# A decoder layer on one Trainium2 core: its opening stage in a new order, with part of the w_mod sums on TensorE

## The chip, the core and the metric

One core of one Trainium2 chip runs the whole program. The metric is the device time of one execution in microseconds; a kernel's time is the median of several runs. Traces come from one profiled execution each, whose own time is given beside the runs'.

## The reference

One decoder layer for 256 tokens of width 2048, all in float32:

```python
c_act = silu(c)
mod = c_act @ w_mod + b_mod                      # (2048) @ (2048, 6*2048)
shift1, scale1, gate1, shift2, scale2, gate2 = split(mod, 6)
u = rms(x, norm1_w) * (1 + scale1) + shift1
proj = u @ w_in                                  # 18464 columns
# stick-breaking attention and gated DeltaNet from proj, merged by gates, w_out, then
u = rms(h, norm2_w) * (1 + scale2) + shift2
h = h + gate2 * ((silu(u @ w_gate) * (u @ w_up)) @ w_down)
```

What matters here is the start: no column of `proj` can be computed before a part of u is known, and a part of u needs x, its row norm, and the columns of shift1 and scale1 that belong to it, each a sum over all 2048 rows of w_mod.

## The kernel before

All large products are made on TensorE from a high and a low part: an operand is split into a float32r value (hi) and the rest (lo), and a product is hi·hi + lo·hi + hi·lo, three matmuls. The weights are read in loads `raw` of 512 KB (two K tiles of 128 rows by 512 columns) on SP's queue, the first two on SP and the next two on POOL (L297 to L312). ScalarE makes `wh` from a load (`split_hi`, L302), VectorE `wl` (`split_lo`, L307). Four buffers of each stand ready; the load for step n+4 is issued behind wl of step n. A step is one such load: two K tiles of one job, 24 matmuls. A job is 512 columns of one weight over all its K tiles.

The first jobs need u by K tiles, and u comes in four pieces of four K tiles (`PIECES`). So they run K outermost (`outer`, L985 and around): first three jobs over K tiles 0 to 7, whose sums are then parked in SBUF (`park`, L955; 12 steps), then three other jobs over all 16 K tiles (24 steps). A hook of the first job of each group calls `u_piece(pi)` (L492): pieces 0 and 1 at K tiles 0 and 4 of the first group, 2 and 3 at K tiles 8 and 10 of the second (`HK` is by how many tiles a hook comes early).

For one piece, `u_sums` (L413) goes through 16 blocks of w_mod: 128 rows by 512 columns of shift and 512 of scale, 512 KB each, loaded on POOL's queue into nine buffers `smod` (`load_smod`, L397, L407), up to eight ahead. VectorE adds each block, times its 128 values of c, to one of two accumulators in turn, acc01 and accb (the first two blocks by a plain multiply, L425, the others by L427 with the helper of L124). Then TensorE sums over the partitions: a matmul of each 128 accumulator columns with 64 columns of ones (`pb_mod`, L429 to L436), two of a piece's four column groups at a time, and three small VectorE steps make `mcols`, the scale and shift columns. `u_piece` applies them on ScalarE to xT (x normed and transposed), casts to uh on ScalarE, takes ul on VectorE (L498 to L504), and at once makes the piece's share of b and a (`pb_ba`).

In program order the opening is: constants and the small rows (L134 to L154), silu(c), the sums of blocks 0 to 3 (`NS0`), then the loads of x (`xs`, L447), `wba` (L449, 2048 rows of 128 bytes), `crow` (L451), `adt` (L453), the transposes of crow and their copy `cw` (L457 to L461), the squares of x, the root `rstd1` on POOL (L173), the scaling of x on VectorE (L471), the sums of blocks 4 to 7 (`NS1`), the transposes of x and their copies (L479, L480), the split of wba.

The order on each engine isn't the program's: the framework's scheduler lists the instructions per engine by its own picture of when they become ready, and goes by program order among those that are ready. `tc.keep_in_program_order(ins)` pins an instruction behind the one that was written before it on the same engine. Each engine takes its list in order. `tps`, `wp`, `big` and `ps` are pools of buffers; `bank` gives one of four PSUM banks of tag ms.

The 16 blocks' sums of the next piece are spread over the steps (in `run_jobs`):

```python
if n < n_outer and sums:
    next(sums[0], None)
    if tick % 3 == 0:
        next(sums[0], None)
```

Of the kernel before, what the change touches and what calls it, by code (L numbers as in the profile page):

```python
# [16 lines left out]
P = 128  # L17
# [21 lines left out]
H2 = 5  # L39
RG = 2  # L40
SMA = 8
NS0 = 4
NS1 = 4
PIECES = ((0, 4), (4, 4), (8, 4), (12, 4))
HK = (0, 0, 0, 2)
HOP = 3
LAG = 6
SBR = 16
# [49 lines left out]
def body(tc, cst, x, c, w_mod, b_mod, norm1_w, w_in, q_norm_w, k_norm_w, conv_w, a_log, dt_bias,  # L98
# [19 lines left out]
        nc.tensor.matmul(o, lhsT=lhsT, rhs=rhs, start=start, stop=stop, skip_group_check=True)  # L118

    def tt(o, a, b, op):  # L120
        nc.vector.tensor_tensor(out=o, in0=a, in1=b, op=op)  # L121

    def stt(o, a, s, b, op0, op1, **kw):
        nc.vector.scalar_tensor_tensor(out=o, in0=a, scalar=s, in1=b, op0=op0, op1=op1, **kw)  # L124

    def act(o, i, f, **kw):
        nc.scalar.activation(out=o, in_=i, func=f, **kw)

    def f32(t):
        return t.bitcast(F32)  # L130
# [158 lines left out]
    def run_jobs(jobs, bg_every=0, outer=(), bg_from=0):  # L289
# [11 lines left out]

        def split_hi(n):  # L302
            wh = wp.tile([P, 2, 512], F32R, tag="wh", name="wh", bufs=WB)
            nc.scalar.copy(out=wh, in_=raws[n])  # L304
            splits[n] = (wh,)

        def split_lo(n):  # L307
            wl = wp.tile([P, 2, 512], F32R, tag="wl", name="wl", bufs=WB)
            wh = splits[n][0]
            tt(wl, raws.pop(n), f32(wh), ALU.subtract)  # L310
            if n + RAWS < ns:
                load(n + RAWS)  # L312
            splits[n] = (wh, wl)
# [79 lines left out]

    loads = [(pi, g) for pi, (k0, kn) in enumerate(pieces) for g in range(KT * kn // 4)]
    smod = {}

    def load_smod(n):  # L397

        for i in [i for i in loads if i not in smod][:max(0, n - len([i for i in smod if smod[i] is not None]))]:
# [10 lines left out]
                    nc.gpsimd.dma_start(out=t[:, v], in_=src[:, v, :, c0:c0 + cn])  # L410
            smod[i] = t

    def u_sums(pi):  # L413
        k0, kn = pieces[pi]
        c0, cn = k0 * P, kn * P
        kg = 4 // kn
        for g in range(KT // kg):
            load_smod(SMA)
            t = smod[pi, g]
            smod[pi, g] = None  # L420
            for kk in range(kg):
                k = kg * g + kk
                a = (acc01, accb)[k % 2][:, :, c0:c0 + cn]
                if k < 2:
                    nc.vector.tensor_scalar(out=a, in0=t[:, :, kk], scalar1=cc[:, k:k + 1], scalar2=None, op0=ALU.mult)  # L425
                else:
                    stt(a, t[:, :, kk], cc[:, k:k + 1], a, ALU.mult, ALU.add)  # L427
            yield
        for i0 in range(0, kn, 2):  # L429
            pm = bank("pb_mod")  # L430
            for n in range(2):
                for i in range(2):
                    o = pm[:, 64 * (4 * n + i):64 * (4 * n + i + 1)]
                    sl = slice(c0 + (i0 + i) * P, c0 + (i0 + i + 1) * P)
                    mm(o, acc01[:, n, sl], ones[:, 0:64], True, False)
                    mm(o, accb[:, n, sl], ones[:, 0:64], False, True)  # L436
            kr = slice(k0 + i0, k0 + i0 + 2)
            tt(mcols[:, 0, kr], pm[:, 256:384:64], bsc1[:, kr], ALU.add)
            stt(mcols[:, 0, kr], mcols[:, 0, kr], 1.0, n1c[:, kr], ALU.add, ALU.mult)
            tt(mcols[:, 1, kr], pm[:, 0:128:64], bsh1[:, kr], ALU.add)  # L440
        yield

    sums = [u_sums(0)]
    for _ in range(NS0):
        next(sums[0])
    xs = big.tile([P, NB, D], F32, tag="s16", name="xs")
    nc.sync.dma_start(out=xs, in_=xv)  # L447
    wba = tps.tile([P, KT, 32], F32, name="wba")
    nc.sync.dma_start(out=wba, in_=w_in[:, OFF_BA:OFF_BA + 32].rearrange("(k p) n -> p k n", p=P))  # L449
    for i in range(2):  # L450
        nc.sync.dma_start(out=crow[:, i], in_=conv_w.rearrange("a (k p) -> (a k) p", p=P)[i * 96:(i + 1) * 96])  # L451
    adt = cp.tile([P, 2, H], F32, name="adt")
    nc.sync.dma_start(out=adt[:, 0], in_=a_log.partition_broadcast(P))  # L453
    nc.sync.dma_start(out=adt[:, 1], in_=dt_bias.partition_broadcast(P))

    cw = cp.tile([P, 2, 96], F32, name="cw")
    pc = bank("pb_cw")  # L457
    for i in range(2):
        nc.tensor.transpose(pc[:, i * 96:(i + 1) * 96], crow[:, i], ident[:96, :96])
    nc.vector.tensor_copy(out=cw, in_=pc[:, 0:192])  # L460
    cwv = cw.rearrange("p a b -> p (a b)")  # L461

    ss = cp.tile([P, 4, 8], F32, name="ss")
    xT = s16("xT")
    rstd1 = cp.tile([P, 2], F32, name="rstd1")
    for b in range(NB):
        act(xT[:, b * 8:(b + 1) * 8].rearrange("p k t -> p (k t)"), xs[:, b], AF.Square, accum_out=ss[:, 0, b:b + 1])
    nc.vector.tensor_scalar(out=ss[:, 1, 0:2], in0=ss[:, 0, 0:2], scalar1=1.0 / D, scalar2=EPS, op0=ALU.mult, op1=ALU.add)
# [22 lines left out]

    def u_piece(pi):  # L492
        k0, kn = pieces[pi]
        for _ in sums.pop():
            pass
        if pi + 1 < len(pieces):
            sums.append(u_sums(pi + 1))
        for k in range(k0, k0 + kn, 2):  # L498
            for i in range(2):
# [5 lines left out]
        if not pba:  # L505
# [904 lines left out]
```

## Time and profile before

| | |
|---|---|
| time, median of 3 runs | 2054.28 us (2053.36 to 2054.73) |
| the profiled execution: time | 2056.12 us |
| its span | 2054.1 us |
| TensorE busy (matmul) | 1983.1 us, 97% |
| VectorE busy | 1386.4 us, 67% |
| ScalarE busy | 1064.9 us, 52% |
| GpSimd busy | 108.9 us, 5% |
| mean granted TensorE clock | 0.99 |
| DMA | 449.72 MB, mean 219 GB/s |

How to read it: the rows further down come from one profiled execution. PE is TensorE's matmuls, PEld its weight loads, DVE VectorE, ACT ScalarE, POOL GpSimd, SP SyncE; a name with q behind it is that engine's instruction queue, where DMAs are issued. Starts and windows are microseconds from the span's start. L118 and the like are lines of the kernel; L118, L121, L124 and L127 are the helpers for matmul, tensor-tensor, scalar-tensor-tensor and activation, so a group is told apart by its operands. In square brackets stands how long the engine had been idle and what ended that. One fp32 matmul with ones appears as two records.

### The profile page before, as it was taken

The page shows a single profiled execution, that of the slowest core. Times are in us where ns is not written, and L with a number is a line of the kernel's source. Part 1 is how long each engine was busy: PE and PEld are TensorE (multiplying, and loading weights), DVE is VectorE, ACT ScalarE, POOL GpSimd, SP SyncE. Part 2 cuts the span into 40 slices and gives each one's busy share as a digit, 9 for nine tenths or more (in the row PEclk, how much of TensorE's full clock was granted, in tenths as well). Part 3 has the DMA queues.
Part 4 walks back from the last instruction along what each step waited for, and adds up shares of the span by engine and source line. Part 5 has one row for each costly group of instructions (what it writes and reads, how often), then busy time and mean ns, then how long its engine had stood idle before and what let it go on. Part 6 is the DMA issues. An engine that isn't in the chain of part 4 may idle for free.

```text
span 2054.1 us, 29271 instructions
## 1 busy us (share of the span) xinstructions
PE 1983.1 (97%) x11097; PEld 1720.7 (84%) x11097; DVE 1386.4 (67%) x1846; ACT 1064.9 (52%) x1766; POOL 108.9 (5%) x141
## 2 busy tenths in 40 slices
PE   1999999999999999999999999999999999999998
PEld 1899999897888888888888888788888888888887
DVE  4986979877676667447776877676775555556554
ACT  3346676776666667443454445554455334445432
POOL 4311011010000000000000000000000000000000
PEclk9899999999999999999999999999999999999999
DMA  8995533444776675768797888587875566665564
GB/s 302 386 336 184 160 126 116 125 122 142 240 229 197 223 232 165 222 193 284 253 309 257 301 320 277 178 269 239 268 244 185 195 193 188 188 189 186 186 214 134
DMA packets 208555, 449.72 MB, mean 219 GB/s; under 512 B 16103, under 2 KB 16538, under 8 KB 207902
## 3 DMA queue, kind: packets, MB, share of 16 engines
q1 hardware_dynamic: 198910, 413.25, 62.6%
q0 software_dynamic: 9504, 34.61, 4.5%
q8 instruction: 87, 1.43, 0.3%
q14 instruction: 54, 0.44, 0.1%
HBM read 445.70 MB, written 2.10 MB: 218 GB/s over the span
## 4 chain that ended last, share of the span: by engine, by line
PE 93%; DMA 3%; DVE 2%; issue 1%; ACT 1%; POOL 0%; SPq 0%; DVEq 0%; ACTq 0%; POOLq 0%
PE acc L118 85%; DMA smod<-in_w_mod 1%; DMA crow<-in_conv_w 1%; PE pb_mod L118 1%; PE pb_Q L118 1%; DMA raw<-in_w_in 0%; PE pb_oa L118 0%; PE pb_z L118 0%; PE pb_X L118 0%; DVE wl L121 0%; PE pb_af L118 0%; DVE accb L124 0%; PE pb_o L118 0%; PE pb_u L118 0%; PE pb_tr L140 0%
## 5 line engine op out<-in xcount | busy, mean ns | idle before, releaser
L121 DVE TENSOR_TENSOR wl<-raw,wh 128x1024 fp32r<-128x1024 f32 x648 | 791.8, 1224 | 515.4 <-ACT wh L304 513.8
L304 ACT CAST wh<-raw 128x1024 fp32r<-128x1024 f32 x648 | 680.2, 1050 | 776.7 <-PE acc L118 694.9
L118 PE MATMUL acc<-u,wh 128*128 128x512 f32 x1408 | 494.8, 396 | 0.0
L118 PE MATMUL acc<-u,wl 128*128 128x256 f32 x1408 | 395.3, 281 | 0.0
L118 PEld LDWEIGHTS acc<-u,wh 128*128 128x128 f32 x1408 | 264.2, 188 | 63.1
L118 PE MATMUL acc<-wh,uh 128*128 128x512 f32 x768 | 307.1, 400 | 0.0
L118 PE MATMUL acc<-wl,uh 128*128 128x512 f32 x768 | 300.6, 391 | 0.0
L118 PE MATMUL acc<-wh,ul 128*128 128x512 f32 x768 | 300.1, 391 | 0.0
L118 PEld LDWEIGHTS acc<-u,wl 128*128 128x128 f32 x1408 | 266.1, 189 | 0.2
L118 PE MATMUL acc<-uh,wh 128*128 128x256 f32 x768 | 221.3, 291 | 1.5 <-ACT part L955 1.5
L118 PE MATMUL acc<-ul,wh 128*128 128x256 f32 x768 | 218.8, 286 | 0.0
L118 PE MATMUL acc<-uh,wl 128*128 128x256 f32 x768 | 218.7, 286 | 0.0
L118 PE MATMUL acc<-wh,ff 128*128 128x512 f32 x704 | 216.9, 389 | 0.0
L118 PEld LDWEIGHTS acc<-wl,uh 128*128 128x128 f32 x768 | 144.5, 188 | 30.8
L118 PEld LDWEIGHTS acc<-wh,ul 128*128 128x128 f32 x768 | 144.8, 189 | 27.2
L118 PEld LDWEIGHTS acc<-wh,uh 128*128 128x128 f32 x768 | 144.7, 188 | 26.8
L118 PEld LDWEIGHTS acc<-wh,ff 128*128 128x128 f32 x704 | 132.0, 188 | 27.5
L118 PEld LDWEIGHTS acc<-uh,wh 128*128 128x128 f32 x768 | 148.6, 195 | 2.6 <-ACT part L955 1.7
L118 PEld LDWEIGHTS acc<-ul,wh 128*128 128x128 f32 x768 | 148.6, 193 | 0.6
L118 PEld LDWEIGHTS acc<-uh,wl 128*128 128x128 f32 x768 | 148.0, 193 | 0.4
L118 PE MATMUL acc<-wl,ff 128*128 128x512 f32 x352 | 137.0, 389 | 0.0
L202 DVE SCALAR_TENSOR_TENSOR macc<-wm,cols,macc 128x1024 f32<-128x1024 f32 x92 | 117.7, 1280 | 0.8 <-DMA wm<-in_w_mod 0.6
(289 smaller groups left out, 2269.2 us busy)
## 6 DMA issues: line engine op xcount, KB each, us to landing
raw<-in_w_in SPq DMA_DIRECT2D x286, 512.0 KB, 4.2
wm<-in_w_mod SPq DMA_DIRECT2D x128, 512.0 KB, 5.6
raw<-in_w_gate SPq DMA_DIRECT2D x88, 512.0 KB, 4.5
raw<-in_w_up SPq DMA_DIRECT2D x88, 512.0 KB, 4.4
raw<-in_w_down SPq DMA_DIRECT2D x88, 512.0 KB, 4.3
smod<-in_w_mod POOLq DMA_DIRECT2D x64, 512.0 KB, 11.4
raw<-in_p_a SPq DMA_DIRECT2D x32, 512.0 KB, 4.9
raw<-in_p_b SPq DMA_DIRECT2D x32, 512.0 KB, 5.0
```

Source lines behind the costliest of these rows:

```text
L118: nc.tensor.matmul(o, lhsT=lhsT, rhs=rhs, start=start, stop=stop, skip_group_check=True)
L121: nc.vector.tensor_tensor(out=o, in0=a, in1=b, op=op)
L202: ins = nc.vector.scalar_tensor_tensor(out=acc, in0=t, scalar=cc[:, k:k + 1], in1=acc, op0=ALU.mult, op1=ALU.add)
L304: nc.scalar.copy(out=wh, in_=raws[n])
```

## The change

x is loaded first, in two DMAs, and squared, scaled (now on ScalarE) and transposed before blocks 6 to 13 are summed; the small loads and what is made of them move into `u_piece` and a new `ba_piece`, one piece later each. In the first two pieces (`PEP`) every third block (`PEM`) isn't added by VectorE but multiplied on TensorE straight into the bank `pm`, one column per 128 columns. All column sums of a piece go into that one bank, with one column of ones instead of 64. uh is written by ScalarE in one pass with scale and shift, while VectorE makes the shifted xT anew and ul from it. Many instructions are pinned. The third hook comes four K tiles earlier. The helpers tt, stt and act now return their instruction.

```diff
-NS0 = 4
-NS1 = 4
+NS0 = 6
+NS1 = 8
+PEP = 2
+PEM = 3
-HK = (0, 0, 0, 2)
+HK = (0, 0, 4, 2)
...
         def split_hi(n):
-            nc.scalar.copy(out=wh, in_=raws[n])
+            ins = nc.scalar.copy(out=wh, in_=raws[n])
+            if outer and n < 2:
+                pin(ins)
...
         def split_lo(n):
-            tt(wl, raws.pop(n), f32(wh), ALU.subtract)
+            ins = nc.vector.tensor_tensor(out=wl, in0=raws.pop(n), in1=f32(wh), op=ALU.subtract)
+            if outer and n < 2:
+                pin(ins)
...
+    pin = tc.keep_in_program_order
...
+    def by_pe(pi, k):
+        return pi < PEP and k % PEM == PEM - 1
+
     def u_sums(pi):
...
+        pm = bank("pb_mod")
+        col = lambda n, i: pm[:, n * kn + i:n * kn + i + 1]
+        blk = lambda i: slice(c0 + i * P, c0 + (i + 1) * P)
+        first, used = True, 0
...
-                a = (acc01, accb)[k % 2][:, :, c0:c0 + cn]
-                if k < 2:
-                    nc.vector.tensor_scalar(out=a, in0=t[:, :, kk], scalar1=cc[:, k:k + 1], scalar2=None, op0=ALU.mult)
+                if by_pe(pi, k):
+                    for n in range(2):
+                        for i in range(kn):
+                            mm(col(n, i), t[:, n, kk, i * P:(i + 1) * P], cc[:, k:k + 1], first, False)
+                            first = False
+                    continue
+                a = (acc01, accb)[used % 2][:, :, c0:c0 + cn]
+                if used < 2:
+                    ins = nc.vector.tensor_scalar(out=a, in0=t[:, :, kk], scalar1=cc[:, k:k + 1], scalar2=None, op0=ALU.mult)
                 else:
-                    stt(a, t[:, :, kk], cc[:, k:k + 1], a, ALU.mult, ALU.add)
+                    ins = nc.vector.scalar_tensor_tensor(out=a, in0=t[:, :, kk], scalar=cc[:, k:k + 1], in1=a, op0=ALU.mult, op1=ALU.add)
+                pin(ins)
+                used += 1
             yield
-        for i0 in range(0, kn, 2):
-            pm = bank("pb_mod")
+        for a in ((acc01, accb) if used % 2 else (accb, acc01))[::-1]:
             for n in range(2):
-                for i in range(2):
-                    o = pm[:, 64 * (4 * n + i):64 * (4 * n + i + 1)]
-                    mm(o, acc01[:, n, sl], ones[:, 0:64], True, False)
-                    mm(o, accb[:, n, sl], ones[:, 0:64], False, True)
...
+                for i in range(kn):
+                    mm(col(n, i), a[:, n, blk(i)], ones[:, 0:1], first, a is (acc01, accb)[(used + 1) % 2])
+                    first = False
+        kr = slice(k0, k0 + kn)
+        pin(tt(mcols[:, 0, kr], pm[:, kn:2 * kn], bsc1[:, kr], ALU.add))
...
+    xs = big.tile([P, NB, D], F32, tag="s16", name="xs")
+    for b in range(NB):
+        nc.sync.dma_start(out=xs[:, b], in_=xv[:, b])
     sums = [u_sums(0)]
     for _ in range(NS0):
         next(sums[0])
-    nc.sync.dma_start(out=xs, in_=xv)
...
-        nc.vector.tensor_scalar(out=xs[:, b], in0=xs[:, b], scalar1=rstd1[:, b:b + 1], scalar2=None, op0=ALU.mult)
-    for _ in range(NS1):
-        next(sums[0])
+        pin(act(xs[:, b], xs[:, b], AF.Copy, scale=rstd1[:, b:b + 1]))
...
-        nc.scalar.copy(out=xT[:, 2 * j:2 * j + 2], in_=pt.rearrange("p (a t) -> p a t", t=T))
+        pin(nc.scalar.copy(out=xT[:, 2 * j:2 * j + 2], in_=pt.rearrange("p (a t) -> p a t", t=T)))
+    for _ in range(NS1):
+        next(sums[0])
...
+    def small_loads():
+        nc.sync.dma_start(out=wba, in_=w_in[:, OFF_BA:OFF_BA + 32].rearrange("(k p) n -> p k n", p=P))
+        for i in range(2):
+            nc.sync.dma_start(out=crow[:, i], in_=conv_w.rearrange("a (k p) -> (a k) p", p=P)[i * 96:(i + 1) * 96])
...
+    def small_splits():
+        pin(nc.scalar.copy(out=wbah, in_=wba))
+        pin(tt(wbal, wba, f32(wbah), ALU.subtract))
+        pc = bank("pb_cw")
...
+        pin(nc.vector.tensor_copy(out=cw, in_=pc[:, 0:192]))
...
     def u_piece(pi):
+        if pi:
+            ba_piece(pi - 1)
         for _ in sums.pop():
             pass
...
-            for i in range(2):
-                act(xT[:, k + i], xT[:, k + i], AF.Identity, scale=mcols[:, 0, k + i:k + i + 1],
-                    bias=mcols[:, 1, k + i:k + i + 1])
-            nc.scalar.copy(out=uh[:, k2], in_=xT[:, k2])
-            tt(ul[:, k2], xT[:, k2], f32(uh[:, k2]), ALU.subtract)
+            for i in range(k, k + 2):
+                act(uh[:, i], xT[:, i], AF.Identity, scale=mcols[:, 0, i:i + 1], bias=mcols[:, 1, i:i + 1])
+            for i in range(k, k + 2):
+                pin(nc.vector.tensor_scalar(out=xT[:, i], in0=xT[:, i], scalar1=mcols[:, 0, i:i + 1],
+                                            scalar2=mcols[:, 1, i:i + 1], op0=ALU.mult, op1=ALU.add))
+            pin(tt(ul[:, k2], xT[:, k2], f32(uh[:, k2]), ALU.subtract))
+        if pi == 0:
+            small_loads()
+
+    def ba_piece(pi):
+        if pi == 0:
+            small_splits()
             pba.append(bank("pb_ba"))
+        k0, kn = pieces[pi]
         o = pba[0][0:32, 0:T]
...
     def gdn_scalars():
+        ba_piece(len(pieces) - 1)
-        act(ea, adt[:, 0], AF.Exp)
+        pin(act(ea, adt[:, 0], AF.Exp))
```

## Rows read from the trace of the kernel before

**Rows 1.** Stretches: start:end, length, busy us (instructions) per engine, granted clock, DMA share, GB/s.

```profile
0.00:32.00 32.00, 1.05 (x3) 0.55 (x3) 9.69 (x13) 6.29 (x8) 10.74 (x21) 1.00 0.96 325
32.00:40.00 8.00, 0.00 (x0) 0.00 (x0) 8.00 (x9) 4.77 (x6) 3.92 (x5) 1.00 0.43 136
40.00:56.00 16.00, 10.61 (x64) 9.93 (x64) 10.42 (x16) 8.49 (x14) 8.77 (x12) 1.00 1.00 365
56.00:108.00 52.00, 48.13 (x350) 46.36 (x350) 48.58 (x50) 17.85 (x24) 21.25 (x30) 0.87 1.03 386
56.00:60.00 4.00, 3.76 (x19) 3.33 (x20) 4.00 (x5) 1.31 (x3) 1.10 (x2) 0.57 1.03 387
80.00:90.00 10.00, 8.89 (x43) 8.18 (x42) 7.14 (x14) 4.21 (x7) 2.33 (x5) 0.51 1.03 387
115.00:181.00 66.00, 66.00 (x556) 65.81 (x554) 47.65 (x50) 28.75 (x37) 7.52 (x13) 1.00 0.86 293
181.00:2054.00 1873.00, 1850.81 (x10073) 1591.57 (x10071) 1258.61 (x1704) 995.63 (x1677) 55.59 (x61) 0.99 0.65 208
```

**Rows 2.** The chain that ended last, 0 to 200 us: start, us, what.

```profile
4.86 20.98 DMA crow<-in_conv_w
...
39.83 9.98 DMA smod<-in_w_mod
...
64.35 12.80 DMA smod<-in_w_mod
...
80.86 3.66 PE pb_mod L118 x16
...
96.72 10.10 DMA raw<-in_w_in
...
159.62 1.74 PE pb_mod L118 x16
```

**Rows 3.** Timeline of the opening: start, us, engine, line, operation [idle before, releaser].

```profile
4.86 12.87 SPq L451 DMA_DIRECT2D crow<-in_conv_w  x2
...
20.37 0.70 SPq L447 DMA_DIRECT2D xs<-in_x  x1
...
26.53 0.36 DVE L460 COPY cw<-pb_cw 128x192 f32<-128x192 f32 x1 [12.85 <-PE pb_cw L459]
...
28.38 0.72 POOL L407 DMA_DIRECT2D smod<-in_w_mod  x1 [13.68 <-DVE acc L124]
...
31.00 1.91 ACT L127 ACTIVATE xT<-xs 128x2048 f32<-128x2048 f32 x1 [4.55 <-DMA xs<-in_x]
...
36.08 1.60 POOL L173 TENSOR_TENSOR rstd<-ss,half 128x2 f32<-128x2 f32 x1 [6.98 <-DVE ss L468]
...
43.10 6.95 PE L140 MATMUL pb_u<-cs,xs 128*128 128x128 f32 x32 [16.61 <-DVE xs L471]
...
49.91 1.28 DVE L124 SCALAR_TENSOR_TENSOR accb<-smod,cols,accb 128x1024 f32<-128x1024 f32 x1 [3.41 <-DMA smod<-in_w_mod]
...
56.45 1.49 PE L118 MATMUL acc<-uh,wh 128*128 128x256 f32 x6
...
107.87 1.55 ACT L955 COPY part<-acc 128x512 f32<-128x512 f32 x3
```

**Rows 4.** DMA queues, 56 to 108 us: packets, MB, share of 16 engines.

```profile
q0 software_dynamic: 4096, 14.91, 75.6%
q1 hardware_dynamic: 2634, 5.10, 27.2%
```

**Rows 5.** Instruction groups up to 170 us: count, busy us, mean ns, idle before.

```profile
L121 DVE TENSOR_TENSOR wl<-raw,wh 128x1024 fp32r<-128x1024 f32 x33 | 40.1, 1223 | 8.1 <-ACT wh L304 8.1
L124 DVE SCALAR_TENSOR_TENSOR acc<-smod,cols,acc 128x1024 f32<-128x1024 f32 x28 | 35.9, 1281 | 1.0 <-DMA smod<-in_w_mod 1.0
L425 DVE TENSOR_SCALAR acc<-smod,cols 128x1024 f32<-128x1024 f32 x4 | 3.0, 747 | 0.0
L121 DVE TENSOR_TENSOR mcols<-pb_mod,cols 128x2 f32<-128x2 f32 x16 | 1.8, 155 | 10.1 <-PE pb_mod L118 9.9
...
L127 ACT ACTIVATE xT<-xT,mcols 128x256 f32<-128x256 f32 x16 | 9.0, 596 | 8.4 <-DVE mcols L124 8.3
```

More of the change, by code (lines that the diff above doesn't have):

```diff
@@ L120, in tt @@
     def tt(o, a, b, op):
-        nc.vector.tensor_tensor(out=o, in0=a, in1=b, op=op)
+        return nc.vector.tensor_tensor(out=o, in0=a, in1=b, op=op)
     def stt(o, a, s, b, op0, op1, **kw):
-        nc.vector.scalar_tensor_tensor(out=o, in0=a, scalar=s, in1=b, op0=op0, op1=op1, **kw)
+        return nc.vector.scalar_tensor_tensor(out=o, in0=a, scalar=s, in1=b, op0=op0, op1=op1, **kw)
     def act(o, i, f, **kw):
-        nc.scalar.activation(out=o, in_=i, func=f, **kw)
+        return nc.scalar.activation(out=o, in_=i, func=f, **kw)
     def f32(t):
@@ L440, in u_sums @@
-            tt(mcols[:, 1, kr], pm[:, 0:128:64], bsh1[:, kr], ALU.add)
+                for i in range(kn):
[3 more added lines that the diff above has]
+        pin(tt(mcols[:, 0, kr], pm[:, kn:2 * kn], bsc1[:, kr], ALU.add))
+        pin(stt(mcols[:, 0, kr], mcols[:, 0, kr], 1.0, n1c[:, kr], ALU.add, ALU.mult))
+        pin(tt(mcols[:, 1, kr], pm[:, 0:kn], bsh1[:, kr], ALU.add))
@@ L445, in body @@
         next(sums[0])
-    xs = big.tile([P, NB, D], F32, tag="s16", name="xs")
-    nc.sync.dma_start(out=xs, in_=xv)
-    wba = tps.tile([P, KT, 32], F32, name="wba")
-    nc.sync.dma_start(out=wba, in_=w_in[:, OFF_BA:OFF_BA + 32].rearrange("(k p) n -> p k n", p=P))
-    for i in range(2):
[L451 to L461, printed above, removed]
     ss = cp.tile([P, 4, 8], F32, name="ss")
@@ L466, in body @@
     for b in range(NB):
-        act(xT[:, b * 8:(b + 1) * 8].rearrange("p k t -> p (k t)"), xs[:, b], AF.Square, accum_out=ss[:, 0, b:b + 1])
-    nc.vector.tensor_scalar(out=ss[:, 1, 0:2], in0=ss[:, 0, 0:2], scalar1=1.0 / D, scalar2=EPS, op0=ALU.mult, op1=ALU.add)
+        pin(act(xT[:, b * 8:(b + 1) * 8].rearrange("p k t -> p (k t)"), xs[:, b], AF.Square, accum_out=ss[:, 0, b:b + 1]))
+    pin(nc.vector.tensor_scalar(out=ss[:, 1, 0:2], in0=ss[:, 0, 0:2], scalar1=1.0 / D, scalar2=EPS, op0=ALU.mult, op1=ALU.add))
     rsqrt(rstd1, ss[:, 1, 0:2])
     for b in range(NB):
-        nc.vector.tensor_scalar(out=xs[:, b], in0=xs[:, b], scalar1=rstd1[:, b:b + 1], scalar2=None, op0=ALU.mult)
-    for _ in range(NS1):
-        next(sums[0])
+        pin(act(xs[:, b], xs[:, b], AF.Copy, scale=rstd1[:, b:b + 1]))
     for j in range(KT // 2):
@@ L479, in body @@
                 tr(pt[:, i * T + b * P:i * T + (b + 1) * P], xs[:, b, k * P:(k + 1) * P])
-        nc.scalar.copy(out=xT[:, 2 * j:2 * j + 2], in_=pt.rearrange("p (a t) -> p a t", t=T))
+        pin(nc.scalar.copy(out=xT[:, 2 * j:2 * j + 2], in_=pt.rearrange("p (a t) -> p a t", t=T)))
+    for _ in range(NS1):
+        next(sums[0])
+    wba = tps.tile([P, KT, 32], F32, name="wba")
+    adt = cp.tile([P, 2, H], F32, name="adt")
+    cw = cp.tile([P, 2, 96], F32, name="cw")
+    cwv = cw.rearrange("p a b -> p (a b)")
+    def small_loads():
+        nc.sync.dma_start(out=wba, in_=w_in[:, OFF_BA:OFF_BA + 32].rearrange("(k p) n -> p k n", p=P))
+        for i in range(2):
+            nc.sync.dma_start(out=crow[:, i], in_=conv_w.rearrange("a (k p) -> (a k) p", p=P)[i * 96:(i + 1) * 96])
+        nc.sync.dma_start(out=adt[:, 0], in_=a_log.partition_broadcast(P))
+        nc.sync.dma_start(out=adt[:, 1], in_=dt_bias.partition_broadcast(P))
+    def small_splits():
+        pin(nc.scalar.copy(out=wbah, in_=wba))
+        pin(tt(wbal, wba, f32(wbah), ALU.subtract))
+        pc = bank("pb_cw")
+        for i in range(2):
+            nc.tensor.transpose(pc[:, i * 96:(i + 1) * 96], crow[:, i], ident[:96, :96])
+        pin(nc.vector.tensor_copy(out=cw, in_=pc[:, 0:192]))
     wbah = tps.tile([P, KT, 32], F32R, name="wbah")
     wbal = tps.tile([P, KT, 32], F32R, name="wbal")
-    nc.scalar.copy(out=wbah, in_=wba)
-    tt(wbal, wba, f32(wbah), ALU.subtract)
     uh, ul = s16("uh", F32R), s16("ul", F32R)
```

6 lines of the change are left out of this document (removed).

## The prediction

> **What bounds the kernel now.** I read the table of stretches first [rows 1], then the chain of waits [rows 2], then the timeline of the opening [rows 3], then what the two DMA queues and the single instructions cost [rows 4, 5]. The reader is to see a kernel of two parts. From 115 us on TensorE is busy without a gap (66.00 of 66.00 us, then 1850.81 of 1873.00); the change touches nothing there but a few small instructions, so a microsecond is won only ahead of 115 us, and one won there is kept. Ahead of it TensorE waits: its first main matmul starts at 56.45 us [rows 3], and the first twelve steps (a step is two K tiles of one job, 512 KB of w_in, 24 matmuls) end about 107.9 us, when the last half job is parked [rows 3]. That is 51 us, 4.3 a step; of the steps that follow, 556 matmuls take 66.00 us [rows 1], 0.119 each, so 2.9 a step.
>
> Why it waits has three causes. One: the small loads. crow stands on SP's queue for 12.87 us behind wba, cw's copy on VectorE waits for it 12.85 us and stops the sums, so that no buffer of a w_mod block comes free and POOL's next block issue stands 13.68 us; x is issued only at 20.37 and used at 31.00; rstd, in POOL's order ahead of further block loads, comes at 36.08 [rows 3]. So the DMA engines run dry: 136 GB/s in 32 to 40 us, 325 before, against 386 from 56 to 108 [rows 1]. Two: from 56 to 108 us the DMA engines are full (share 1.03) and VectorE almost (48.58 of 52.00): the second and third pieces' sums (1.28 us each, 16 a piece) and the low parts wl (1.22 us) [rows 1, 5]. Three: the chain shows the waits for w_mod blocks at 39.83 and 64.35, for w_in at 96.72, and the column sums pb_mod between them [rows 2].
>
> **The change, part by part.** Sums go against the profiled execution, 2056.12 us (span 2054.1, 2.0 around it), which is 1.84 us above the median 2054.28; the predicted figure is the median less the gain.
>
> *x first.* Two DMAs take the place of crow and wba, issued at about 4.9 us instead of 20.37. How soon x lands beside a full block queue no row shows. Least: alone at 386 GB/s, 2.1 MB take 5.4 us, so 12 us with the delay of a start. Most: with the share that w_in had in 56 to 108, 5.10 MB in 52 us or 98 GB/s [rows 4], 21 us, so 27 us. I take 16: x's own row, issue to first use, 10.6 us [rows 3], and it keeps its place there behind unfinished small loads.
>
> Weighed against a rule: row 4 gives w_mod 14.91 MB in 4096 packets (3.6 KB) and w_in 5.10 MB in 2634 (1.9 KB), so bytes follow packet size rather than halves. The Trainium skill, DMA: Bandwidth & Descriptors, section Queues, rings and completion order, says that an engine goes round its queues packet by packet, so a queue's bytes follow its packets' size; by that x, with longer rows than w_in, would beat the 27 us, and the first main matmul would hardly wait for x; by the byte share it would start about 49 us. The sum below uses neither.
>
> *The way of x to TensorE.* Squares 2 x 1.91, rstd 1.60 [rows 3], the scaling now on ScalarE (2 x 1.91, by the same row), the transposes 6.95 with their copies beside them, two high parts (2.1, two of the ACT rows' kind), wl 1.22: 20 us after 16, so 36. The pinned order puts the last sum of piece 0 behind wl, so both must be there. POOL's rstd stands behind 14 block loads, of which the last needs VectorE's fourth sum, the fifth block: with x 4.7 MB, 13 us at 365 GB/s after a start of 3, and the sum, so 18 us, before x's squares are done.
>
> *The last block of piece 0.* 16 blocks (8.39 MB), x (2.10), four w_in loads (2.10), constants: 12.7 MB. At 365 GB/s, the rate of 40 to 56 us [rows 1], 35 us, after a start of about 3: 38 us, against 49.8 now (39.83 + 9.98 [rows 2]). Between 35 and 41 by which w_in loads go ahead.
>
> *From it to the first main matmul.* Sum 1.28, eight column sums of 0.109 x 2 records (1.74 us for 16 [rows 2]), three VectorE steps of 0.16, the high part in one ScalarE pass, 0.6 [rows 5]: 4.1 us instead of 6.5 now (49.91 to 56.45). First main matmul at 42, a gain of 14 us there.
>
> *Every third block on TensorE.* Five blocks a piece, eight one-column matmuls each, two records a matmul as in the pb_mod rows: 16 x 0.109 = 1.7 us a block, 8.7 a piece. One column instead of 64 could cost anything from nothing to that; I take it whole, since the weights loaded are the same 128 columns. In piece 0 idle TensorE covers it; in piece 1 its wait for w_mod (the 12.80 us row). Uncovered it is 8.7 us. It takes 6 us from VectorE in each of the two pieces. A block matmul that waits for its block holds the main matmuls behind it, but step 6 can't begin before that piece's last block anyway.
>
> *What the DMA engines give back.* Blocks and w_in through step 12 come as before. By 108 us 37.4 MB had come (325 x 32 + 136 x 8 + 365 x 16 + 386 x 52). The hole of 32 to 40 filled is 2.0 MB, 5.2 us; of the 1.95 MB missing in 0 to 32 I let half come back, 2.5 us, as the rest is the start. So with the same bytes all is 7.7 us earlier: piece 1's last block at 69.4 instead of 77.15, step 6 at 73.5. VectorE then has 16 sums of piece 2 (none on TensorE; 19.4 us, two of them plain multiplies at 0.75), about 4.4 wl (5.4) and the low parts of u (2.4): 27 us, so 100.7. Both say that step 12 starts at about 100, not 108: **of the 14 us of the opening some 6 are given back.** Upper end: 3.3 of the 37.4 MB was ahead of need (48 blocks, 12 w_in loads, x and the small loads are 34.1), 8.5 us, so up to 14 could stay. Lower end: nothing stays.
>
> *Small loads late.* On SP's queue behind x and the first w_in loads; nothing needs wba or crow until the second piece's hook at about 70 us, so even the 21 us of crow's row are covered. Uncovered, w_in loads behind them would be late by that.
>
> *After step 12.* The second piece's b and a matmuls move from waiting to busy TensorE: 12 x 0.12 = +1.4 us. Banks: pm stands for a whole piece, so with v's two and pb_ba's one no spare is left; the matmuls that would wait for one come after the copy that frees it, price 0. HK 4 puts the third hook at step 18 and so the fourth piece's 16 sums into steps 18 to 24, pinned: VectorE 27 us beside 18.6 us of matmuls and 1.4 + 3.5 of TensorE's own, 4 us over. Three steps of finished wl (8.6 us) cover that; if not, 4 to 9 us.
>
> Sum: 7.7 from the DMA engines, +1.7 because less is loaded ahead (a fifth of the 8.5), -1.4: **8 us gained, 2046.3.**
>
> **Rivals.**
> 1. *x isn't first in fact.* For it: SP's order now has x behind the small loads though the program has it ahead of them. Then x lands at 31, its 20 us end at 51, first main at 54.5, and POOL's order holds loads behind rstd until 36 again; half the hole stays: gain 2, 2052.3. Against: no sum stands ahead of x any more.
> 2. *The opening's 14 us stay.* The condition is that little is loaded ahead; TensorE's five blocks less on VectorE speak for it, the full DMA row against: 2040.
> 3. *The pins of the fourth piece* cost their 4 to 9 us, since wl isn't ahead: gain 8 less 6, 2052.
> 4. *Slower: TensorE's clock.* After a gap the granted clock was half, 1.2 GHz: 0.57 in 56 to 60 after the wait for u, 0.51 in 80 to 90 after the wait at 77 [rows 1]; pb_mod cost 3.66 for 16 records instead of 1.74 [rows 2]. Block matmuls make TensorE work in short bursts with waits between, from 10 us to 70. If all twelve steps ran at 1.2 GHz they would take 69 us, the block and column matmuls 24: step 12 at 135, 27 us late, 2081. It decides once more than some 40 us of the 66 between 42 and 108 are at the low clock (each costs half a microsecond, and 21 us are slack); 14 are now. Against: the clock came back inside both rows. The Trainium skill, TensorE: Matmul & The Clock Gate, section HAM oscillation, describes just that: bursts shorter than the DMA wait between them start slow each time. The trace agrees that a gap comes before each fall; that it repeats no run here shows.
>
> **How the numbers follow.** Forecast 0.60 (2042 to 2050), rival 1 0.13, rival 2 0.10, rival 3 0.10, rival 4 0.07. A change of 0.2%, 4.1 us, is about what a measurement of this kernel can tell from none. Faster by more: forecast, rival 2 and a little of rival 3, 0.72; within: rivals 1 and 3 and the forecast's edge, 0.20; slower 0.08. Range 2039.5 to 2053: from rival 2 to rivals 1 and 3, leaving out rival 4 and the tails.
>
> **What would show it.** Right: x used about 16 us, no hole in the DMA row before 100 us, first main matmul near 42, a wait for blocks until about 69, the last parked copy near 100, no idle TensorE in 110 to 170. Wrong: x issued behind wba; low clock over 40 us; waits for wl between steps 18 and 27; a last parked copy at 108 although the first main matmul was early.

## The result and the profile after

The changed kernel takes 2064.64 us (2063.97 to 2066.44), beside 2053.83 us for the kernel before on the same chip: a ratio of 1.0053 (95% interval 1.0036 to 1.0071). It is **slower by 10.8 us**, where 8 us less were forecast. The profiled execution took 2064.24 us, its span 2062.5. Two of the runs further down each had one far slower execution (5117 and 2478 us), which is left out of their medians.

First the stretches of the changed kernel, with the columns of [rows 1]:

```profile
0.00:32.00 32.00, 12.47 (x56) 11.97 (x56) 9.71 (x12) 12.35 (x11) 14.91 (x27) 1.00 0.94 340
32.00:40.00 8.00, 8.00 (x42) 8.00 (x43) 2.57 (x2) 3.44 (x7) 4.51 (x7) 1.00 1.06 363
40.00:56.00 16.00, 14.34 (x78) 13.96 (x77) 7.13 (x13) 6.90 (x11) 2.17 (x3) 0.58 1.00 353
56.00:108.00 52.00, 52.00 (x402) 51.09 (x401) 41.98 (x46) 15.35 (x20) 19.55 (x28) 0.90 0.93 334
80.00:90.00 10.00, 10.00 (x49) 9.13 (x49) 4.39 (x10) 2.08 (x4) 1.98 (x3) 0.51 1.01 365
115.00:181.00 66.00, 59.97 (x487) 59.28 (x487) 47.21 (x54) 23.28 (x28) 7.65 (x13) 0.97 0.75 247
```

The hole of 32 to 40 us is filled (363 GB/s instead of 136). But 56 to 108 us moves 334 GB/s where it moved 386, although TensorE is busy without a gap there; and 115 to 181 us, full before, now has 6 us of idle TensorE. Next the chain of waits:

```profile
16.76 13.86 DMA smod<-in_w_mod
30.67 3.58 PE pb_mod L120 x16
34.25 6.08 PE pb_u L142 x32
40.33 11.17 PE pb_mod L120 x64
...
77.81 7.75 PE pb_mod L120 x48
...
118.81 8.36 DMA raw<-in_w_in
...
140.61 10.25 DMA raw<-in_w_in
```

Against [rows 2] the two waits for w_mod between 39 and 77 us are gone; block matmuls, transposes and column sums on TensorE stand in their place. The timeline of the opening shows how:

```profile
4.45 1.05 SPq L467 DMA_DIRECT2D xs<-in_x  x2
...
14.80 1.91 ACT L129 ACTIVATE xT<-xs 128x2048 f32<-128x2048 f32 x1 [5.98 <-DMA xs<-in_x]
...
20.03 3.58 PE L120 MATMUL pb_mod<-cols,smod 128*128 128x1 f32 x16 [5.01 <-DMA smod<-in_w_mod]
...
21.77 3.89 ACT L129 ACTIVATE xs<-xs,rstd 128x2048 f32<-128x2048 f32 x2 [1.12 <-POOL rstd L175]
...
30.02 2.88 POOL L414 DMA_DIRECT2D smod<-in_w_mod  x4 [4.59 <-PE pb_mod L120]
...
34.11 6.22 PE L142 MATMUL pb_u<-cs,xs 128*128 128x128 f32 x32
...
44.52 3.55 PE L120 MATMUL pb_mod<-cols,smod 128*128 128x1 f32 x16
47.93 3.55 PE L120 MATMUL pb_mod<-cs,acc 128*128 128x1 f32 x16
...
51.52 0.16 DVE L123 TENSOR_TENSOR mcols<-pb_mod,cols 128x4 f32<-128x4 f32 x1 [5.93 <-PE pb_mod L120]
...
52.70 1.22 PE L120 MATMUL acc<-uh,wh 128*128 128x256 f32 x4 [1.22 <-ACT uh L129]
```

x is used at 14.80 us instead of 31.00 [rows 3] and scaled by 25.66. Its transposes start at 34.11 only: in TensorE's queue they stand behind four blocks' matmuls, each of which came when its block landed and took 3.55 us. Even a block of piece 1 (44.52) stands ahead of piece 0's last column sums. The first main matmul comes at 52.70, 3.8 us earlier than before.

To see what becomes of that I count steps (24 main matmuls each, from the records of every trace). Start in the kernel before, and what each run is later (+) or earlier (-):

| step | before | after | no blocks | order free | neither | halves | hook at own k | hook one k early |
|---|---|---|---|---|---|---|---|---|
| 0 | 56.45 | -3.8 | -10.2 | -2.8 | -5.5 | -6.7 | -5.1 | -3.8 |
| 5 | 73.58 | +1.0 | -9.4 | +3.1 | -3.5 | -4.9 | -5.2 | -3.5 |
| 6 | 84.52 | +3.4 | +0.3 | +1.9 | -1.1 | -6.0 | -5.0 | -3.3 |
| 11 | 103.29 | +0.5 | -1.4 | -0.6 | -2.6 | -6.0 | -6.2 | -4.2 |
| 14 | 117.19 | +1.3 | -1.7 | +9.2 | -1.2 | -1.9 | -4.6 | -2.7 |
| 21 | 137.35 | +1.3 | -1.7 | +9.8 | -1.2 | -1.9 | -4.6 | -2.7 |
| 31 | 172.45 | +8.2 | +6.9 | +11.7 | +0.2 | +3.1 | -2.7 | -2.7 |
| 38 | 193.47 | +9.5 | +8.3 | +13.0 | +1.6 | +4.5 | -1.3 | -1.3 |

The columns are runs below. Each column is one execution, and executions of one kernel differ by some us (2052.26 to 2064.24 in the run "neither"), so a difference of a few us between columns counts only where rows show what it comes from. The changed kernel loses its lead in steps 1 to 6, and 6.9 us more in steps 21 to 31.

### The profile page after: what moved, and what is told of

The parts are those of the page before. It is cut to its first block, busy times and chain, and to the rows that moved or that the text cites. A ratio compares the mean times of both kernels' runs of the same rounds, so it can differ in the third digit from the quotient of the medians.

```text
span 2062.5 us, 29574 instructions
## 1 busy us (share of the span) xinstructions
PE 2011.6 (98%) x11257; PEld 1750.4 (85%) x11257; DVE 1376.1 (67%) x1838; ACT 1067.4 (52%) x1762; POOL 106.4 (5%) x141
## 4 chain that ended last, share of the span: by engine, by line
PE 92%; DMA 2%; DVE 2%; issue 2%; ACT 2%; POOL 0%; DVEq 0%; ACTq 0%; POOLq 0%
PE acc L120 83%; PE pb_mod L120 2%; DMA smod<-in_w_mod 1%; DMA raw<-in_w_in 1%; PE pb_Q L120 1%; PE pb_u L142 1%; DVE wl L314 1%; PE pb_oa L120 0%; ACT wh L306 0%; PE pb_z L120 0%; PE pb_X L120 0%; PE pb_af L120 0%; PE pb_o L120 0%; PE pb_u L120 0%; PE pb_tr L142 0%
```

## The experiments

All edits are to the changed kernel if nothing else is said. A ratio is to the kernel before on the same chip, with its 95% interval; a median is of 4 to 12 runs.

### Blocks, order, hook, each undone alone

No matmuls on blocks of w_mod:

```diff
-PEP = 2
+PEP = 0
```

> The change with no block summed on TensorE (PEP 0, so VectorE adds all 16 blocks of every piece). Theory A, the block matmuls are what eats the early start: the transposes of x no longer wait behind them (they stood from 25.7 to 34.1), the first main matmul comes before 48 us instead of 52.7, step 6 before 84 instead of 88, and the total is 2056 to 2060; the stall between steps 21 and 26 stays (about 7 us). Rival B, the transfers of w_mod set the pace whoever adds: first main and step 6 within 2 us of the change's, total 2063 to 2066.

2062.68 us, ratio 1.0035 (1.0021 to 1.0049), not Theory A's 2056 to 2060. The early start is there: the first main matmul is 10.2 us earlier. It is all given back at step 6, as this timeline of the run shows:

```profile
38.06 3.54 PE L120 MATMUL pb_mod<-cs,acc 128*128 128x1 f32 x16 [7.46 <-DVE acc L448]
41.46 3.55 PE L120 MATMUL pb_mod<-cs,accb 128*128 128x1 f32 x16
...
68.02 0.30 PE L120 MATMUL pb_ba<-uh,wbah 128*32 128x256 f32 x1 [3.19 <-ACT wbah L504]
...
74.75 0.42 PE L120 MATMUL pb_ba<-uh,wbal 128*32 128x256 f32 x1 [3.91 <-DVE wbal L123]
...
76.89 3.40 PE L120 MATMUL pb_mod<-cs,acc 128*128 128x1 f32 x16
80.16 3.55 PE L120 MATMUL pb_mod<-cs,accb 128*128 128x1 f32 x16
...
88.81 1.44 POOL L414 DMA_DIRECT2D smod<-in_w_mod  x2 [14.84 <-DVE acc L446]
```

All 32 records of a piece's column sums now stand ahead of its first u and take 7 us (granted clock 0.50 in 78 to 84 us). Ahead of those of the second piece TensorE waits 3.19 and 3.91 us for the two parts of wba, which ScalarE and VectorE make behind other work, and makes ten b/a matmuls, 2.1 us. The next piece's first sum is kept behind the columns and u on VectorE, so for 14.84 us no buffer of a block comes free.

Blocks in the first piece alone:

```diff
-PEP = 2
+PEP = 1
```

> The change with blocks on TensorE in the first piece alone (PEP 1). Theory A: the first main matmul stays at 52 to 54 us, but steps 0 to 5 lose their three bursts of block matmuls and the two at the end, so step 6 starts 3 to 6 us earlier than 88, if VectorE with 5 more sums (6 us) keeps up; total 2059 to 2063. Rival B: step 6 at 88, total 2064.

2064.32 us, ratio 1.0045 (1.0032 to 1.0057); step 0 is 5.9 us earlier than before, step 6 3.2 later (with the blocks 3.4) and step 31 10.8 later. Not to be told from the changed kernel, as Rival B has it.

VectorE's order of the sums kept in the first piece only:

```diff
-                pin(ins)
+                if pi < 1:
+                    pin(ins)
```

> The change with the sums of pieces 1 to 3 not pinned (only those of piece 0 are). Theory A, the pinned sums of the fourth piece stand ahead of wl on VectorE from step 18 on: the 7 to 8 us lost between steps 21 and 29 vanish, total 2056 to 2058. Rival B, the waits there are for w_in transfers that share the queues with w_mod: still lost, total 2063 to 2066.

2062.93 us, ratio 1.0041 (1.0028 to 1.0053), where Theory A said 2056 to 2058. Steps 21 to 31 lose 1.9 us instead of 6.9, but steps 12 to 14 lose 6.6 that they didn't.

The third hook as before:

```diff
-HK = (0, 0, 4, 2)
+HK = (0, 0, 0, 2)
```

> The change with the third hook where it was (HK 0 0 0 2), pins kept. If the early hook is what puts the fourth piece's sums in the way, the 7 us come back: total 2057. If the pins are, the same 16 sums now stand pinned in three steps, 24 to 27, instead of nine, and the stall grows: 15 us or more between steps 24 and 29, total 2070 or more.

2063.91 us, ratio 1.0047 (1.0033 to 1.006), less than the 2070 that was expected of the pins. Up to step 29 it is 1.95 us ahead of before; then the fourth piece's sums, kept in order, end so late that 12.3 us are lost at one step. TensorE waits 3.27 us for the last of them, and the column sums behind it take 7 us (granted clock 0.50 in 168 to 178 us) with nothing beside them:

```profile
168.64 3.54 PE L120 MATMUL pb_mod<-cs,acc 128*128 128x1 f32 x16 [3.27 <-DVE acc L448]
172.04 3.55 PE L120 MATMUL pb_mod<-cs,accb 128*128 128x1 f32 x16
```

None of these four parts alone carries the 10.8 us.

### Two or more undone; x alone

No blocks, sums free behind piece 0, hook as before (`PEP = 0`, `HK = (0, 0, 0, 2)`, and the `if pi < 1` above):

> The changed kernel without matmuls on w_mod's blocks, with the sums kept in program order in the first piece only and the third piece's hook where it was before; x first, late small loads, one column per sum and the one-pass high part stay. Theory P (the sums of pieces 2 to 4 kept in program order stand ahead of the wl that TensorE waits for, and keep the next blocks from loading): the lead of 9.4 us at step 5 that the run without blocks showed is now kept, about 2045 us (2043 to 2049). Rival B (the loads of w_mod and w_in bound steps 6 to 14, so any lead of the opening is given back there): 2051 to 2055. Rival C (the one-column sums at the end of each piece, in one pass with TensorE at its low clock, cost what is lost): 2056 to 2062.

2061.0 us, ratio 1.0026 (1.0015 to 1.0036). Theory P, as stated for the sums, misses its range by 12 us; the time lies in C's. The same with the blocks left in (`PEP = 2`):

> The changed kernel with the sums kept in program order in the first piece only and the third piece's hook as before; the matmuls on w_mod's blocks stay. Theory P: the stalls of steps 12 to 14 (6.6 us, hook) and of steps 21 to 30 (pins) both go, which leaves the lead that the changed kernel has in front (4 to 8 us at the first step, most of it given back in step 6 while the blocks' matmuls run at the low clock): 2050 to 2056. Rival B: 2052 to 2055 as well, so the pair with the run without blocks decides: under P it is 3 us or more slower than that one, under B within 2 us of it. Rival C: 2057 to 2063.

2062.67 us, ratio 1.0033 (1.0021 to 1.0046): 1.7 us above its twin, not the 3 that P asks for, and in C's range; the two intervals overlap.

The columns and u's operations on VectorE free as well (run "neither" of the table):

```diff
+    pin0 = lambda pi, ins: pin(ins) if pi < 1 else ins
...
-        pin(tt(mcols[:, 0, kr], pm[:, kn:2 * kn], bsc1[:, kr], ALU.add))
+        pin0(pi, tt(mcols[:, 0, kr], pm[:, kn:2 * kn], bsc1[:, kr], ALU.add))
...
```

> As the run without blocks and with the sums in program order in the first piece only, but the three column operations and the two operations on u of pieces 2 to 4 are not kept in program order either. If only the sums' place costs (theory P as stated): the same as that run within 1 us. If the place of every later operation on VectorE costs (P extended): 2 to 5 us faster than that run. Rivals B and C: no difference.

2056.21 us, ratio 1.0007 (0.9996 to 1.0018), 4.8 us below the first run of this group (the two intervals just overlap): the place of every later VectorE operation counts, not that of the sums alone. So I freed all of them in the changed kernel itself, sums, columns and u, with blocks and hook left ("order free"):

> The changed kernel with one edit: behind the first piece neither the sums nor the columns nor the operations on u are kept in program order on VectorE; block matmuls, hooks, the columns' form and everything else stay. Theory P in its wide form (the place of every later VectorE operation of pieces 2 to 4): most of the 10.8 us goes, 2055 to 2059, with the stall of steps 21 to 29 (6.85 us) gone and steps 12 to 14 within 2 us of the changed kernel's. If sums alone were the matter: 2062 to 2063, as in the run that freed only them. If the block matmuls and the columns' form carry the loss: 2061 to 2065.

2064.07 us, ratio 1.0037 (1.0025 to 1.0049). The wide form of P misses its time too: steps 21 to 31 lose 1.8 us instead of 6.9, but steps 12 to 14 lose 9.8, where the run had been 0.6 us ahead of before. Most of that is TensorE's clock. The same stretch of the kernel before and of this run, and the wait in it:

```profile
105.00:128.00 23.00, 21.54 (x183) 21.34 (x182) 16.53 (x23) 11.33 (x17) 4.34 (x6) 1.00 1.03 379
```

```profile
105.00:128.00 23.00, 20.16 (x107) 19.85 (x106) 11.52 (x15) 6.67 (x10) 3.61 (x5) 0.63 0.81 295
...
109.31 0.39 PE L120 MATMUL acc<-uh,wh 128*128 128x256 f32 x1 [2.84 <-ACT part L994]
```

At a granted clock of 0.63 instead of 1.00, 23 us lose 8.5 (an estimate: 0.37 of 23). The same stretch stands at 0.78 in the run with the sums free in pieces 2 to 4, which lost 6.6 us there. What lets the clock fall isn't settled: here TensorE had waited 2.84 us for a bank, while in the run "neither" (0.85) it waited for nothing from 96 us on.

Blocks without the order: 2064. Order without blocks: 2062.7. Neither (and the old hook): 2056.2. **Undoing one of the two leaves most of the loss; undoing both, and the hook, takes most of it away.** That the blocks alone are enough is not shown, as the run with the order free lost its time at the low clock behind the last block; and as the hook was never kept with both undone, its part is open.

What the two do to the loads is in the waits of POOL's queue in the changed kernel (total us, times, longest): for TensorE from 10 to 90 us, then the two largest of 56 to 108 us, then two stretches.

```profile
POOL smod L414 <- PE pb_mod L120: 36.4, 10, 7.3
...
POOL smod L414 <- DVE acc L446: 16.7, 2, 9.9
POOL smod L414 <- PE pb_mod L120: 13.0, 4, 4.1
...
56.00:60.00 4.00, 4.00 (x34) 4.00 (x33) 4.00 (x5) 1.06 (x2) 1.80 (x3) 0.95 0.45 146
92.00:96.00 4.00, 4.00 (x36) 4.00 (x35) 4.00 (x5) 1.57 (x2) 2.76 (x4) 1.00 0.68 217
```

A block that TensorE is to sum keeps its buffer until TensorE's queue comes to it. Most of the 36.4 us fell before 56 us, where the rate held. The 52 GB/s that are missing behind it have two sources: 13.0 us of waiting for block matmuls, and 16.7 us, in two waits, for the plain multiply that begins a piece's sums (L446) and is kept behind columns and u. The lowest rates, 146 and 217 GB/s, stand at the end of the latter two. In the run with neither, POOL waited for no TensorE instruction at all from 10 to 90 us, and 56 to 108 us moved 385 GB/s.

The other half of the question, x first alone, on the kernel before:

```diff
-    nc.sync.dma_start(out=xs, in_=xv)
...
+    for b in range(NB):
+        nc.sync.dma_start(out=xs[:, b], in_=xv[:, b])
     sums = [u_sums(0)]
```

> The kernel before with one edit: x's two loads issued ahead of the first blocks of w_mod; the small loads stay where they were, the sums stay as they were. Theory P: x is worked at 16 us, the first main matmul comes at about 46 us instead of 56.4, and as nothing is pinned most of it stays: 2045 to 2049. Rival B (transfers bound steps 6 to 14): 2051 to 2055 with the lead gone by step 14. Rival D (the last blocks of piece 1 set the start, so x first alone moves nothing in front): first main matmul at 54 or later and 2053 to 2055.

2053.99 us, ratio 0.9996 (0.9987 to 1.0004): no change, first main matmul at 59.7, as Rival D has it. x is used at 14.38, but the transposes still start at 41.6, as VectorE's scaling of x stays behind its sums. The early x alone is worth nothing while the scaling stands there; what ScalarE's scaling and the new order are worth singly, no run shows.

### What gives the lead back

From here the frame is the run "neither", to see what becomes of a lead with neither burden. First the b/a matmuls of the piece before behind u instead of ahead of the column sums; then also the columns in two halves with a bank each ("halves"):

```diff
-        if pi:
-            ba_piece(pi - 1)
         for _ in sums.pop():
...
+        else:
+            ba_piece(pi - 1)
```

```diff
+        for i0 in range(0, kn, 2):
+            pm, first = bank("pb_mod"), True
...
```

> The run without later pins (no block matmuls, VectorE's order kept in the first piece only, hook as before) with one further edit: the 12 b/a matmuls of the piece before, and the splits of their small weights, come behind this piece's columns and u instead of ahead of its column sums. There step 5 to 6 took 10.36 us, with 2.39 us of waiting for the small splits and 1.3 us of these matmuls ahead of the column sums. Theory T (what stands between a piece's last sum and its first main matmul sets steps 0, 6 and 13): step 6 comes 2 to 4 us earlier, the whole 2052 to 2055. Rival B (w_mod's transfers set steps 6 and 13): no difference, 2055 to 2057. Under both the first main matmul stays at 51.

> As the run with the b/a matmuls behind the columns, and the columns in two halves of two, each in its own bank, as in the kernel before. Theory T: 1.5 to 3 us are gained at steps 0, 6 and 13, as the first half's u is worked on beside the second half's sums; the first main matmul at 48 to 49.5 us, step 6 at 78 to 80, and 2048 to 2052 in all, so faster than before by 1 to 3 thousandths. Rival B: the start moves by 2 us but step 13 and all behind it stay within 1 us of the kernel before: 2053 to 2056.

2058.39 us, ratio 1.0018 (1.0009 to 1.0027), and 2058.32, ratio 1.0019 (1.001 to 1.0028). Theory T is right on the steps and neither theory on the time: step 6 comes 5 and 6 us earlier than before, and step 11 6 us; then most of the lead is lost. The kernel before, the first of these runs and the run "hook at own k" show the same thing at step 12:

```profile
106.92 1.04 ACT L304 CAST wh<-raw 128x1024 fp32r<-128x1024 f32 x1 [1.89 <-DMA raw<-in_w_in]
...
108.50 0.39 PE L118 MATMUL acc<-uh,wh 128*128 128x256 f32 x1 [1.46 <-ACT part L955]
```

```profile
99.80 1.04 ACT L306 CAST wh<-raw 128x1024 fp32r<-128x1024 f32 x1 [4.45 <-DMA raw<-in_w_in]
100.76 1.07 ACT L995 COPY part<-acc 128x512 f32<-128x512 f32 x2
...
101.39 0.38 PE L120 MATMUL acc<-uh,wh 128*128 128x256 f32 x1 [2.82 <-ACT part L995]
```

```profile
100.99 1.04 ACT L306 CAST wh<-raw 128x1024 fp32r<-128x1024 f32 x1 [1.88 <-DMA raw<-in_w_in]
...
102.58 0.39 PE L120 MATMUL acc<-uh,wh 128*128 128x256 f32 x1 [1.70 <-ACT part L990]
```

ScalarE waits in order for a w_in load; the copy that frees a bank stands behind it, and TensorE behind the copy. The DMA engines are full there (share 1.00 in 92 to 108 us of the second run shown), so a lead is cut to the pace of the transfers: rival B, in part. The clock takes a share as well: 0.85 in 105 to 128 us in both of these runs, 1.00 before and in the run "hook at own k". The second place is piece 4, in the kernel before and in the run "halves":

```profile
152.67 1.28 DVE L124 SCALAR_TENSOR_TENSOR accb<-smod,cols,accb 128x1024 f32<-128x1024 f32 x1
...
156.00 0.33 PE L118 MATMUL pb_mod<-cs,acc 128*128 128x64 f32 x2
```

```profile
154.04 1.28 DVE L442 SCALAR_TENSOR_TENSOR accb<-smod,cols,accb 128x1024 f32<-128x1024 f32 x1
...
154.27 1.02 PE L120 MATMUL pb_mod<-cs,acc 128*128 128x1 f32 x8 [1.40 <-DVE acc L442]
...
158.88 1.84 PE L120 MATMUL pb_mod<-cs,accb 128*128 128x1 f32 x8
...
160.77 0.23 DVE L123 TENSOR_TENSOR mcols<-pb_mod,cols 128x2 f32<-128x2 f32 x2 [3.75 <-PE pb_mod L120]
```

Before, the last sum started at 152.67 us and TensorE came to the columns at 156.00, after it; here TensorE comes first and waits, and its last eight records take 1.84 us where the first eight took 1.02. The granted clock is 0.80 in 146 to 172 us (1.00 before), worth 5.2 us (an estimate: 0.20 of 26), about the 5.0 that steps 21 to 31 lose.

The same two edits in the changed kernel itself:

> The changed kernel, with all its pins, block matmuls and hooks, but with the columns in two halves and the b/a matmuls of the piece before behind them. Theory T alone: most of the 10.8 us comes back, 2055 to 2058. Theory P and T together (pins for steps 21 to 30, the tail for steps 6 and 13): the tail gives 2 to 4 us at step 6, the stall of steps 21 to 30 (6.85 us) stays: 2060 to 2063. Neither: 2064 to 2065.

2066.3 us, ratio 1.006 (1.0048 to 1.0073): above the 2060 to 2063 of P and T together; the tail isn't what its steps 1 to 6 wait for.

u's high part in two passes as before, in the run with halves, and then with the fourth hook at its own k, and in the changed kernel alone:

```diff
-                act(uh[:, i], xT[:, i], AF.Identity, scale=mcols[:, 0, i:i + 1], bias=mcols[:, 1, i:i + 1])
...
+                act(xT[:, k + i], xT[:, k + i], AF.Identity, scale=mcols[:, 0, k + i:k + i + 1],
...
+            nc.scalar.copy(out=uh[:, k2], in_=xT[:, k2])
```

> As the run with columns in halves and the b/a matmuls behind them (no block matmuls, VectorE's order kept in the first piece only), with the high part written as in the kernel before: ScalarE scales x into place and copies it, VectorE only subtracts. Theory V (VectorE is what sets piece 4: its 16 sums there end at 155 us whatever the lead, and the four scalings of u that moved onto it stand ahead of the first of these sums): piece 4's first sum comes at 117 to 119 instead of 121.6, its last at 151 to 153, the wait of TensorE ahead of piece 4's columns goes, and 3 to 6 us come back: 2051 to 2055. Rival W (piece 4's w_mod transfers, issued late, set it): the last sum stays at 154 to 155 and the time at 2057 to 2059.

> As the run with u in two passes, and the fourth piece's hook at its own first k (three steps later), so that its sums have 8.6 us more before TensorE asks for them. If the wait at piece 4's columns is what gives the lead back: 2048 to 2051, step 30 ahead of the kernel before by 4 to 6 us. If what follows the hook (columns and u with nothing to cover them) costs as much as the wait: 2054 to 2058.

> The changed kernel with one edit undone: the high part of u in two passes as before. Theory V: VectorE gets back 1.5 us a piece; steps 21 to 30, where VectorE is busy without a break, lose 1 to 3 us less: 2061 to 2064. Theory P alone (only the place of the sums matters): 2064 to 2066.

2055.51 us, ratio 1.0001 (0.9992 to 1.001); 2054.05, ratio 1.0003 (0.9994 to 1.0012); 2064.22, ratio 1.0046 (1.0033 to 1.0058). The first is 2.8 us better than one pass (on another chip), half a microsecond off Theory V's range, but not by its way: piece 4's first sum comes at 122.4, not at 117 to 119. In the changed kernel the form of u makes no difference that can be told. With the late hook step 12 starts at 100.0 us and a lead of 4.6 us reaches piece 4; behind the hook, whose columns and u nothing covers, 2.7 are left.

Last, the fourth hook one k early (`HK = (0, 0, 0, 1)`), that with one pass in pieces 1 and 2, and one pass there with the hook at its own k:

> As the run with u in two passes and the fourth hook at its own k, with that hook one k earlier (HK 0, 0, 0, 1). There the lead of 4.6 us of steps 14 to 24 shrank to 2.7 at step 31, as columns and u of piece 4 stood uncovered. Theory V (the lead is lost where TensorE has no work between a piece's last sum and its first u): with a step and a half of cover it stays at 4 to 5 us behind step 31, 2049 to 2052. Rival W (the last sum of piece 4 and its transfers): 2053 to 2055.

> As the run with the fourth hook one k earlier, and the high part written in one pass in pieces 1 and 2 alone, where TensorE waits for u (2.5 us from the columns to the first main matmul of step 6 in the run with halves, 5 to 6 us in the two-pass runs). Theory V: step 6 comes 2 to 3 us earlier, at 77 to 78; if transfers set steps 12 to 14 (rival B) that is gone by step 14, and the time is the run before's within 1 us; if not, 2 us less, 2047 to 2050.

> As the run with the high part in one pass in pieces 1 and 2 alone, and the fourth hook at its own k. Tells the two edits apart: by theory V 1 to 3 us slower than its twin with the hook one k earlier, 2050 to 2053; by rival W equal to it within 1 us.

2052.23 us, ratio 0.9996 (0.9986 to 1.0006); 2052.94, ratio 0.9998 (0.9987 to 1.001); 2054.09, ratio 1.0014 (1.0004 to 1.0024). The hook's cover does keep what reaches it (2.7 us at step 21, 2.7 at step 31), but less came through step 12 than in the run with the late hook; both are 1.3 us ahead at step 38, which is too little to be told. One pass brings step 6 to 6.1 us ahead, 2.7 more, and 0.6 are left at step 14. That isn't rival B alone: in the twin with the hook at its own k, with the same edits up to there, 4.9 are left at step 14, and the granted clock in 105 to 128 us is 1.00 instead of 0.85. The twins' times can't be told apart. **No version beats the kernel before by what can be measured.**

## Why the prediction was wrong

**What held.** x first: used at 14.80 us, forecast 16; so rival 1 falls. The wait for small loads: crow's issue stands 26.32 us on SP's queue and delays nothing on the changed kernel's path (without the blocks the parts of wba did, by 3.19 and 3.91 us). The b/a matmuls cost 1.4 us in steps 31 to 38 of every run with them moved. What the DMA engines give back: step 12 at about 100 was the forecast, and in the run with u in two passes and the late hook it is 100.0; in the changed kernel itself it is 107.2.

**Where the sum went.** 9.4 us were to be won by step 12 (7.7 + 1.7); 1.0 was lost. Behind it only 1.4 was to be lost; that was lost, and 6.9 more in steps 21 to 31.

**The step that failed first**: "in piece 0 idle TensorE covers it; in piece 1 its wait for w_mod". A block was priced at 1.7 us of an idle engine. It took 3.55, and idle time doesn't cover what stands in a queue: x's transposes were ready at 25.66 and began at 34.11. In piece 1 TensorE was busy from step 1 to 5 with main matmuls, so the blocks there were added (4.8 us between steps 0 and 5, where the run without blocks loses 0.8). VectorE's last sum of piece 1 did start 3.2 us earlier (74.08 instead of 77.25), but TensorE came to the column sums only at 79.38, and these took 6 us. The prediction did say that a block matmul holds what is behind it; it missed that it holds its buffer too (36.4 us of POOL's waits).

The Trainium skill, TensorE: Matmul & The Clock Gate, section Architectural detail, says that TensorE's queue can pull weight loads ahead of matmuls in flight. The trace shows no more reordering than that: the transposes, ready for 8.5 us, passed no block matmul.

**The second**: the column sums, "1.74 us for 16". Two accumulators and four column groups of two make 16 matmuls, 32 records, and in one pass all stand ahead of u: 7 us at 0.22. Without blocks the first main matmul came at 46.2, not at 42.

**The third**: "a microsecond is won only ahead of 115 us, and one won there is kept". TensorE was busy behind 115 us because it was late. When it comes earlier, piece 4's sums, spread over VectorE, are not there. The leads of 1.2, 1.9 and 4.6 us at step 21 were a loss of 0.2, a loss of 3.1 and 2.7 at step 31; with the hook one k early one stayed whole. In part the loss was the clock, as shown for the run "halves".

**Rival 3** was right in mechanism and price (4 to 9 us, measured 6.9 between steps 21 and 31), but forecast as covered by wl's lead. It isn't; VectorE of the changed kernel:

```profile
139.37 1.22 DVE L314 TENSOR_TENSOR wl<-raw,wh 128x1024 fp32r<-128x1024 f32 x1
140.50 1.28 DVE L448 SCALAR_TENSOR_TENSOR acc<-smod,cols,acc 128x1024 f32<-128x1024 f32 x1
...
142.90 1.21 DVE L314 TENSOR_TENSOR wl<-raw,wh 128x1024 fp32r<-128x1024 f32 x1
...
147.62 1.21 DVE L314 TENSOR_TENSOR wl<-raw,wh 128x1024 fp32r<-128x1024 f32 x1
...
152.06 0.58 PE L120 MATMUL acc<-uh,wh 128*128 128x256 f32 x1 [4.05 <-ACT wh L306]
```

A wl every 3.5 to 4.7 us, where a step of TensorE takes 2.9; and TensorE's longest wait there, 4.05 us, is for the wh of the load that was issued behind the late wl (140.61 in the chain above). **Rival 4**, the clock, had the right sign; its condition, over 40 us at the low clock, wasn't met. At 0.58 in 40 to 56 us and 0.90 in 56 to 108, some 24 us were (an estimate from the rows), where before had 14. In the changed kernel its price is in the blocks and column sums above; in the run with the order free it was the largest loss.

The Trainium skill, TensorE: Matmul & The Clock Gate, section HAM oscillation, says that bursts shorter than the DMA wait between them start slow each time. The trace agrees on the slow start: the first four blocks took 3.54 to 3.58 us each, three between main matmuls 1.84. But the waits ahead of the four, 0.96 to 5.01 us, were in part shorter than the bursts.

Open: what lets the clock fall in steps 12 to 14 of the changed kernel with its order free. The hook and the blocks weren't parted there; and as free operations are listed anew by the scheduler, each run with fewer pins is also another order.

## What to carry to other kernels

Price a piece of work that moves to another engine by what is queued behind it there and by the buffers that it holds till its turn, not by that engine's idle share. An engine that is busy without a gap is busy in step with its feeders: ask, for each place behind the gain, when the next input is ready, before counting a lead as kept. Look at the granted clock of a stretch before explaining what it lost. Where two parts of a change each cost, undoing one shows little; undo them in pairs too.

## What the runs showed of the hardware

A matmul with one column costs as much as one with 64: 16 records in 1.84 us beside the 1.74 of [rows 2]. The granted clock didn't tell the speed of the opening: it stands at 1.00 from 0 to 40 us, where the four blocks took 3.54 to 3.58 us, about the double of the 1.84 at 40.16 and later on; durations did.
